# Elementwise work and the remainders of weights move from POOL to VectorE in a two-layer decoder trunk on one core

## Chip, cores and metric

One core of a Trainium2 chip runs the kernel alone. The metric is the device time of one launch in microseconds; what is shown is the median of the runs, and beside it one profiled execution with its own time.

## What is computed

One inference step of a trunk of two layers, for a prompt of 1024 tokens and a sample group of 8 x 4 tokens that share all weights. Layer 0 mixes by causal pooling and by sliding-window attention at three dilations, layer 1 by a chunked gMLP gate and a short convolution. Both then have a squared-ReLU MLP (1024 to 4096 to 1024) and a gated input embedding; norms are RMS norms in float32. Cut to what matters here:

```python
for i in range(DEPTH):                                    # DEPTH = 2
    h = rmsnorm(r, norm_mix[i])
    y = even_mixer(h, ...) if i % 2 == 0 else odd_mixer(h, ...)
    r = r + y
    h = rmsnorm(r, norm_ffn[i])
    r = r + square(relu(h @ ffn_w1[i])) @ ffn_w2[i]
    h = rmsnorm(r, norm_ple[i])
    r = r + sigmoid(h @ ple_w_gate[i]) * (p[i] @ ple_w_proj[i])
out = rmsnorm(r, norm_final)
# even_mixer: z = h @ w_in; q and k of each head get rope (x1*cos - x2*sin, x2*cos + x1*sin);
#   attention per dilation group, the three outputs combined by a softmax over their log-sums;
#   y = concat(pooled, attended) @ w_out
# odd_mixer: gelu gate, layer norm and 128-token spatial mix; g_out * conv3(g_in * xin); y = concat @ w_out
```

## The kernel before, in words

All 1056 tokens (1024 of the prompt, 32 of the sample) lie as columns, the features as eight tiles of 128 partitions. A float32 product is made of three passes of TensorE (PE): weights and activations are each split in a high part and a remainder, and the passes are high x high, high x remainder and remainder x high. For an activation the high part `sh` comes from ACT and the remainder `sl` from VectorE (DVE).

**The stream of weights.** `wseq` lists all weight tiles (128x1024) in the order of their use. `w_load` brings one to `wraw` (or to `wr`, where the MLP's weights are first combined for a Winograd-like scheme: L206 to L217 on DVE) by a DMA from SP's queue. `w_split(i)` lets ACT copy the tile rounded to `whi` (L153) and an elementwise engine make the remainder `wlo` = raw - high (L157), and then lets the next load start. `whi` and `wlo` have two buffers each. Before the change L157 stands on POOL (GpSimd) unless `eng` says DVE; in the MLP stages of layers 0 and 1 it stands on DVE two steps after the rounding. `w_ahead` splits the next weight while PE works on the present one, `w_next` takes it.

**Order.** Every engine runs its own instructions in the order in which the code issues them. A step of a product ends in `fill.step()`; `fill.after(n, f)` has `f` issued n steps later. That is how the other work is spread between the steps.

**Stages**, with their times in the profile: layer 0's mixer (0 to 770 us) with its tiles of q, k and v, the rope (`rope_tile`: cos on DVE at L490, sin by `pool_tt` at L284 on POOL, sum at L495 and remains for the sample at L497 and L499), and units of attention (`nmx`, L604, from the row maxima; ACT's exponential `p`, L607; PE's transposes `pt`, L626); the mixer's output product, which also leads into the MLP (770 to 866); the MLP of layer 0 (866 to 1454); its embedding and the input products of layer 1's mixer up to 1650; layer 1's mixer (1650 to 1900), which runs in the same code as an MLP does, in two products (`product1`, L1323, and `product2`, L1484); the lead and the MLP of layer 1 (to 2604); its embedding and the final norm.

In the lead of layer 0, `eo_part2(f)` runs eight times: nine matmuls, the sum `r` (DVE, L1120), the remainder `sl` of the tile before (DVE, L1142), then on ACT the rounding `sh` (L1137) and the square (L248), and the sum of squares `acc` (`prep_sq`: POOL for f = 1 to 6 at L284, DVE for f = 7 at L250). When `acc` is whole, PE sums it over partitions (L273).

In the final embedding `last_next` makes the same kind of sum (L1962), the projection's weight remainder `wpl` is DVE's (L1639), and `final_mul` multiplies by the norm's factor (L2009): of the first two thirds of the columns tiles 3 to 7 on POOL, of the last third tiles 5 to 7.

Of the kernel before, what the change touches and what calls it, by code (L numbers as in the profile page):

```python
# [11 lines left out]
F32 = mybir.dt.float32  # L12
# [45 lines left out]
def _build(nc, tc, A, top):  # L58
# [88 lines left out]
    def w_split(i, eng=None, later=False):  # L147
        if i >= len(wseq) or i in wsp:
            return
        w_raw(i)  # L150
        hi = wpool.tile([128, 1024], F32R, tag="whi", name=nm("whi"))
        raw, lo = wop[i]
        ACT.activation(hi, raw, AF.Copy)  # L153
        wsp[i] = (hi, lo)

        def rest():
            (eng or POOL).tensor_tensor(lo, raw, hi.bitcast(F32), op=ALU.subtract)  # L157
            if i not in wraw:
# [71 lines left out]
    def w_next():  # L230
        i = wptr[0]
        wptr[0] += 1
        w_split(i)
        return wsp[i]

    def w_ahead():
        w_split(wptr[0])
# [45 lines left out]
    def pool_tt(out, a, b, op):  # L283
        POOL.tensor_tensor(out, a, b, op=op)  # L284
# [84 lines left out]
    w_split(1, DVE)  # L369
# [8 lines left out]
    for f in (1, 2):  # L378
        pool_tt(xt[0], xt[0], xt[f], ALU.add)
# [65 lines left out]
    def norm0():  # L445
        tags = ("sA", "sB", "pt")
        norm_finish(lambda c: pa.tile([128, 512], F32, tag=tags[c], name=nm("nb")))
        DVE.tensor_tensor(cosr, cosr, rstd, op=ALU.mult)
        pool_tt(sinr, sinr, rstd, ALU.mult)

    def first_two():
# [4 lines left out]
        for t, k in [(t, k) for k in range(6) for t in range(2)] + [(0, 6), (0, 7), (1, 6), (1, 7)]:  # L456
# [7 lines left out]
            if (t, k) == (0, 7):  # L464
                w_split(2, DVE)
        return pss

    def rope_tile(hp, g, j, pss=None):
# [329 lines left out]
    def combine_items(hp):  # L798
# [274 lines left out]
    def gemm_phase(n, kslots, split, mid, evac, last=None, lead=None, chunks=None, skip=(), order=None,  # L1073
# [23 lines left out]
        w_split(wptr[0] + 1)  # L1097
        evac(1, p1)
        for f in range(2, n):
# [9 lines left out]
            if f not in skip:  # L1109
                w_split(wptr[0] + 1)  # L1110
# [60 lines left out]
    def pair(l, xslots, near, far, extra, gi, parts, more_slots, pieces, lead=None, order=None, spilled=False):  # L1171
# [53 lines left out]
        def sums_of(k):  # L1225
# [5 lines left out]
            def s0():  # L1231
                for f in (k, 4 + k):
                    ACT.activation(R[f], R[f], AF.Copy, scale=g[:, f:f + 1])
                POOL.tensor_tensor(raw7(k), c_, a_, op=ALU.subtract)
# [10 lines left out]
            def s3():  # L1245
                lows[5] = split_half(T5[k], a_, later=True)
                lows[3]()
                POOL.tensor_tensor(raw7(k), b_, a_, op=ALU.subtract)
# [61 lines left out]
        def product1(c, p):  # L1310
            w = w_next()
            first = PROD[p][0]
            for m in range(2):
# [12 lines left out]
                if m == 1:  # L1326
                    if (c, p) == (n1 - 1, 3):
                        second_open()
                    if l == "m":
                        w_split(wptr[0] + 1)  # L1330
# [33 lines left out]
        def after2(n, p, kt):  # L1364
# [5 lines left out]
            elif (p, kt) == (4, 1):  # L1370
                build(SD, H1, 1, range(P.early, 4))
                if n == 0:
                    minus(H0, 1, H1, 1, range(2), POOL)
# [4 lines left out]
            elif (p, kt) == (6, 0):  # L1378
                if n == 0:
                    minus(H0, 1, H1, 1, range(2, 4), POOL)  # L1380
# [92 lines left out]
        def product2(n, p, kt):  # L1473
# [3 lines left out]
            for i_m, m in enumerate(M_ORDER):  # L1477
# [10 lines left out]
                if l == "m":  # L1488
                    if m == 2 and not (last and p == 7 and kt == 1):
                        w_split(wptr[0] + 1)  # L1490
                elif i_m == 2 and not (last and p == 7 and kt == 1):
                    rest = w_split(wptr[0] + 1, DVE, True)
                    if rest:
                        fill.after(2, rest)
# [3 lines left out]
                if last and (p, kt, i_m) in pieces:  # L1498
                    ple_piece(*pieces[p, kt, i_m], POOL if l == "m" else DVE, xp, gi)
# [219 lines left out]
    def mix_parts(st):  # L1719
# [20 lines left out]
        def v_path(i, v, at):  # L1740
# [25 lines left out]
            def tr_s():  # L1766
                V.ps = mbank()
                PE.matmul(V.ps[:32, :128], v[:, NP:NT], C.cen, start=True, stop=True)
                POOL.tensor_tensor(C.wss[:, i, :], C.wss[:, i, :], C.smk, op=ALU.mult)
# [29 lines left out]
            def norm():  # L1799
                DVE.scalar_tensor_tensor(V.s, V.s, V.st[:32, 1, 8:9], V.g, op0=ALU.mult, op1=ALU.mult)  # L1800
                POOL.tensor_tensor(V.n, V.n, V.st[:, 1, 0:8].unsqueeze(2).to_broadcast([128, 8, 128]), op=ALU.mult)
# [4 lines left out]
            def offset():  # L1806
# [5 lines left out]
                POOL.tensor_tensor(V.s, V.s, V.o[:32, :], op=ALU.add)  # L1812
# [25 lines left out]
        def conv(i, hd, c, at, then):  # L1838
# [3 lines left out]
            def s0():  # L1842
                pool_tt(hd, hd, c, ALU.mult)
# [22 lines left out]
            def s4():  # L1866
                pool_tt(c, c, rstd, ALU.mult)
# [83 lines left out]
    def last_next(j):  # L1951
# [5 lines left out]
        else:  # L1957
# [4 lines left out]
            (DVE if f == 7 or (ch == ONE and f > 5) else POOL).tensor_tensor(acc[:, cs], acc[:, cs], sq[:, cs], op=ALU.add)  # L1962
        ACT.activation(r, r, AF.Copy, scale=gains[:, 6, f:f + 1])
        if j == 7:
# [4 lines left out]
            for i in range(8):  # L1969
                fill.after(39 + 1 * i, lambda i=i: final_mul(i, TWO, POOL if i in PO else DVE))  # L1970
# [49 lines left out]
    for i, f in enumerate((5, 0, 1, 6, 2, 3, 7, 4)):  # L2020
        if f >= 5:
            final_mul(f, ONE, POOL)
# [160 lines left out]
```

## Time and profile before

| | |
|---|---|
| median of the runs | 2777.39 us (2776.99 to 2777.65) |
| profiled execution, own time | 2770.68 us |
| its span in the profile | 2768.9 us |
| PE busy | 2650.0 us, 96% |
| DVE busy | 1780.0 us, 64%, 2542 instructions |
| ACT busy | 1118.0 us, 40% |
| POOL busy | 567.3 us, 20%, 270 instructions |

The profiled execution is 6.7 us shorter than the median; its trace is 1.8 us shorter than its own time. A line such as "650.00 1.96 DVE L495 ... [2.35 <-POOL tmp L284]" of the timeline says: start, duration, engine, line of the kernel, result and operands, and in brackets how long the engine had stood idle and what ended that. In the list of waits each line says which instructions of PE waited for which result, the total, how often, and the longest. PEclk is the granted clock of PE as a share of full speed.

### The profile page before, as it was taken

What the parts mean: (1) busy time and instruction counts of PE and PEld (TensorE: products, weight loads), DVE (VectorE), ACT (ScalarE), POOL (GpSimd) and SP (SyncE); (2) the same over time, 40 slices, a digit from 0 to 9 for tenths busy, and PEclk for the clock granted to TensorE, in tenths of its full rate; (3) what the DMA queues carried; (4) which work ended last, traced back from release to release, by engine and by line L of the source; (5) the groups of instructions that cost most, each with busy time, mean ns of one, the idle gap of its engine ahead of it and who ended that gap; (6) DMA issues with size and microseconds to landing.
All of it is one profiled execution on the core that took longest, in us unless ns stands there. A gap on an engine that the chain in (4) does not pass through costs nothing. (4 is left out here: it accounts for less than half of the span.)

```text
span 2768.9 us, 48732 instructions
## 1 busy us (share of the span) xinstructions
PE 2650.0 (96%) x20190; PEld 2563.8 (93%) x20190; DVE 1780.0 (64%) x2542; ACT 1118.0 (40%) x1901; POOL 567.3 (20%) x270
## 2 busy tenths in 40 slices
PE   8999999998989999999999999998999999999996
PEld 7898898987889999999999988988999999999996
DVE  7444435454377667777776465778866767777755
ACT  4333333334154333333354355224533343333543
POOL 3332233222251000000001334546400000000034
PEclk9999999999999999999999999999999999999998
DMA  5224334255644444744412222351254448443112
GB/s 172 75 87 130 105 107 147 84 155 157 193 170 166 138 147 154 278 168 156 148 56 79 77 87 89 88 172 47 85 179 157 149 174 293 135 139 132 55 63 103
DMA packets 159294, 366.52 MB, mean 132 GB/s; under 512 B 46528, under 2 KB 54752, under 8 KB 159072
## 3 DMA queue, kind: packets, MB, share of 16 engines
q1 hardware_dynamic: 158208, 362.59, 39.7%
q8 instruction: 159, 2.61, 0.4%
q10 hardware_dynamic: 864, 0.82, 0.1%
q14 instruction: 63, 0.52, 0.1%
HBM read 245.20 MB, written 105.15 MB: 127 GB/s over the span
## 5 line engine op out<-in xcount | busy, mean ns | idle before, releaser
L157 POOL TENSOR_TENSOR wlo<-wraw,whi 128x1024 fp32r<-128x1024 f32 x99 | 244.0, 2465 | 1875.3 <-ACT whi L153 1832.7
L1323 PE MATMUL PS<-sh,whi 128*128 128x264 f32 x2016 | 413.2, 286 | 17.3 <-DVE tmp L1305 4.8
L1323 PE MATMUL PS<-sh,wlo 128*128 128x264 f32 x2016 | 414.3, 287 | 5.9 <-POOL wlo L157 5.9
L1484 PE MATMUL PS<-sh,whi 128*128 128x264 f32 x2016 | 405.3, 283 | 14.2 <-DVE r L1497 12.8
L1323 PE MATMUL PS<-sl,whi 128*128 128x264 f32 x2016 | 413.9, 287 | 0.0
L1484 PE MATMUL PS<-sl,whi 128*128 128x264 f32 x2016 | 408.5, 284 | 1.2 <-DVE sl L1155 1.2
L1484 PE MATMUL PS<-sh,wlo 128*128 128x264 f32 x2016 | 409.4, 284 | 0.0
L1323 PEld LDWEIGHTS PS<-sh,whi 128*128 128x128 f32 x2016 | 318.1, 190 | 20.9 <-DVE tmp L1305 5.2
L1484 PEld LDWEIGHTS PS<-sh,whi 128*128 128x128 f32 x2016 | 313.8, 188 | 17.1 <-issue 11.0
L153 ACT ACTIVATE whi<-wraw 128x1024 fp32r<-128x1024 f32 x181 | 191.5, 1058 | 338.5 <-PE PS L1484 101.1
L1323 PEld LDWEIGHTS PS<-sh,wlo 128*128 128x128 f32 x2016 | 316.4, 191 | 6.9 <-POOL wlo L157 6.9
L153 ACT ACTIVATE whi<-wr 128x1024 fp32r<-128x1024 f32 x153 | 162.3, 1061 | 394.1 <-PE PS L1484 269.9
L1323 PEld LDWEIGHTS PS<-sl,whi 128*128 128x128 f32 x2016 | 315.0, 190 | 0.0
L421 PE MATMUL g<-sh,whi 128*128 128x352 f32 x888 | 310.2, 349 | 4.2 <-DVE vsn L532 3.0
L1484 PEld LDWEIGHTS PS<-sl,whi 128*128 128x128 f32 x2016 | 310.9, 188 | 1.8 <-DVE sl L1155 1.8
L1484 PEld LDWEIGHTS PS<-sh,wlo 128*128 128x128 f32 x2016 | 311.6, 189 | 0.0
L423 PE MATMUL g<-sh,wlo 128*128 128x352 f32 x888 | 287.5, 324 | 0.1
L422 PE MATMUL g<-sl,whi 128*128 128x352 f32 x888 | 287.0, 323 | 0.0
L157 DVE TENSOR_TENSOR wlo<-wr,whi 128x1024 fp32r<-128x1024 f32 x128 | 156.6, 1223 | 180.1 <-ACT whi L153 180.1
L421 PEld LDWEIGHTS g<-sh,whi 128*128 128x128 f32 x888 | 168.0, 189 | 25.8 <-issue 21.7
L1497 DVE TENSOR_TENSOR r<-r,PS 128x528 f32<-128x528 f32 x252 | 168.9, 698 | 21.1 <-PE PS L1484 21.1
L422 PEld LDWEIGHTS g<-sl,whi 128*128 128x128 f32 x888 | 168.9, 190 | 1.4
(341 smaller groups left out, 4593.3 us busy)
## 6 DMA issues: line engine op xcount, KB each, us to landing
hx<-hop SPq DMA_DIRECT2D x56, 528.0 KB, 4.7
tmp<-hop SPq DMA_DIRECT2D x56, 528.0 KB, 4.7
wr<-in_w SPq DMA_DIRECT2D x56, 512.0 KB, 3.7
hop<-tmp SPq DMA_DIRECT2D x96, 264.0 KB, 4.1
hop<-hx SPq DMA_DIRECT2D x96, 264.0 KB, 3.4
wr<-in_w1q SPq DMA_DIRECT2D x42, 512.0 KB, 4.0
wraw<-in_w_e SPq DMA_DIRECT2D x39, 512.0 KB, 3.4
rscr<-r SPq DMA_DIRECT2D x24, 528.0 KB, 3.2
```

The costliest lines, as they stand in the source:

```text
L153: ACT.activation(hi, raw, AF.Copy)
L157: (eng or POOL).tensor_tensor(lo, raw, hi.bitcast(F32), op=ALU.subtract)
L421: PE.matmul(ps[:, :CH], hi[:, ws], xh[:, cs], start=k == 0, stop=False)
L422: PE.matmul(ps[:, :CH], hi[:, ws], xl[:, cs], start=False, stop=False)
L423: PE.matmul(ps[:, :CH], lo[:, ws], xh[:, cs], start=False, stop=k == 7)
L1323: PE.matmul(ps[:, n, :], a[:, ws], b[:, n * HT // 2:(n + 1) * HT // 2], start=first and k == 0 and i == 0, stop=k == 3 and i == 2, skip_gr ...
L1484: PE.matmul(ps[:, q, :], a[:, ws], b[:, q * HT // 2:(q + 1) * HT // 2], start=first and kt == 0 and k == 0 and i == 0, stop=kt == 1 and k ...
L1497: DVE.tensor_tensor(r, r, ps, op=ALU.add)
```

## The change

Every elementwise instruction that `pool_tt` or POOL by name did in these stages is DVE's (`tt`), and so is every `wlo`. `w_split` gives its remainder back as a function; `w_soon(i, steps)` has it issued some steps after the rounding: four in layer 0's mixer, one in the leads, the output products and the embeddings, two in the two products of an MLP or of layer 1's mixer. `w_next` issues it if it is still due. In layer 1's mixer `product2` splits the next weight after the third block in its order (`i_m == 2`) as the other layers do. POOL keeps memsets and the small edges of the pooling (L916, L918): 34 of its 275 issued rows; DVE's grow from 2412 to 2654. PE's order is unchanged.

```diff
+    wrest = {}
+    def w_soon(i, steps=1):
+        rest = w_split(i, True)
+        if rest:
+            wrest[i] = rest
+            fill.after(steps, lambda: w_finish(i))
+    def w_finish(i):
+        if i in wrest:
+            wrest.pop(i)()
-    def w_split(i, eng=None, later=False):
+    def w_split(i, later=False):
...
         def rest():
-            (eng or POOL).tensor_tensor(lo, raw, hi.bitcast(F32), op=ALU.subtract)
+            DVE.tensor_tensor(lo, raw, hi.bitcast(F32), op=ALU.subtract)
...
         w_split(i)
+        w_finish(i)
         return wsp[i]
-    def w_ahead():
-        w_split(wptr[0])
+    def w_ahead(steps=1):
+        w_soon(wptr[0], steps)
...
             if f == 7 or eng is DVE:
                 DVE.tensor_tensor(acc, acc, sq, op=ALU.add)
             else:
-                pool_tt(acc, acc, sq, ALU.add)
+                tt(acc, acc, sq, ALU.add)
...
-    def pool_tt(out, a, b, op):
-        POOL.tensor_tensor(out, a, b, op=op)
+    def tt(out, a, b, op):
+        DVE.tensor_tensor(out, a, b, op=op)
...
             if c == 0 and k == 6:
-                w_ahead()
+                w_ahead(4)
...
             DVE.tensor_tensor(zs, zs, cosr, op=ALU.mult)
-            pool_tt(zw, zw, sinr, ALU.mult)
+            tt(zw, zw, sinr, ALU.mult)
...
                 if g == 1:
-                    pool_tt(ot, ot, st["cb"], ALU.mult)
+                    tt(ot, ot, st["cb"], ALU.mult)
...
-        w_split(wptr[0] + 1)
+        w_soon(wptr[0] + 1)
...
-                    if l == "m":
-                        w_split(wptr[0] + 1)
-                    else:
-                        rest = w_split(wptr[0] + 1, DVE, True)
-                        if rest:
-                            fill.after(2, rest)
+                    w_soon(wptr[0] + 1, 2)
...
-                    minus(H0, 1, H1, 1, range(2), POOL)
+                    minus(H0, 1, H1, 1, range(2))
...
-            (DVE if f == 7 or (ch == ONE and f > 5) else POOL).tensor_tensor(acc[:, cs], acc[:, cs], sq[:, cs], op=ALU.add)
+            DVE.tensor_tensor(acc[:, cs], acc[:, cs], sq[:, cs], op=ALU.add)
...
-                fill.after(39 + 1 * i, lambda i=i: final_mul(i, TWO, POOL if i in PO else DVE))
+                fill.after(39 + 1 * i, lambda i=i: final_mul(i, TWO, DVE))
...
         if f >= 5:
-            final_mul(f, ONE, POOL)
+            final_mul(f, ONE, DVE)
```

Left out of it: the same exchange at `sinr`, the squares of the input, L1234 and L1248 (`t7r`), L1769, L1801, L1812, the two products of the convolution's stages (L1843, L1867) and the sums of the embedding (L1607).

The order of DVE's instructions shows what comes behind what. In the changed kernel lines carry numbers some 14 higher in the middle of the file (L1120 is L1134 there, L1142 is L1156, L284 is L298, L1497 is L1501, L1155 is L1169, L1362 is L1371) and 4 higher near its end (L2009 is L2013).

DVE in the lead of layer 0, before, from the first sum on:

```order
L1120 TENSOR_TENSOR r_7356<-r_7356,PS 128x1056
L1120 TENSOR_TENSOR r_7357<-r_7357,PS 128x1056
L1142 SCALAR_TENSOR_TENSOR sl_83<-r_7356,gains,sh_82 128x1056
L1120 TENSOR_TENSOR r_7358<-r_7358,PS 128x1056
L1142 SCALAR_TENSOR_TENSOR sl_85<-r_7357,gains,sh_84 128x1056
L1120 TENSOR_TENSOR r_7359<-r_7359,PS 128x1056
L1142 SCALAR_TENSOR_TENSOR sl_87<-r_7358,gains,sh_86 128x1056
```

and now:

```order
L1134 TENSOR_TENSOR r_7356<-r_7356,PS 128x1056
L1134 TENSOR_TENSOR r_7357<-r_7357,PS 128x1056
L1156 SCALAR_TENSOR_TENSOR sl_83<-r_7356,gains,sh_82 128x1056
L298 TENSOR_TENSOR acc<-acc,tmp_7505 128x1056
L1134 TENSOR_TENSOR r_7358<-r_7358,PS 128x1056
L1156 SCALAR_TENSOR_TENSOR sl_85<-r_7357,gains,sh_84 128x1056
L298 TENSOR_TENSOR acc<-acc,tmp_7521 128x1056
L1134 TENSOR_TENSOR r_7359<-r_7359,PS 128x1056
L1156 SCALAR_TENSOR_TENSOR sl_87<-r_7358,gains,sh_86 128x1056
L298 TENSOR_TENSOR acc<-acc,tmp_7546 128x1056
```

Between the remainder of one tile and the sum of the next there is now the sum of squares, which before stood on POOL.

DVE in `product2` of layer 1's mixer, before:

```order
L1155 TENSOR_TENSOR sl_95<-hx_17056,sh_94 128x528
L1155 TENSOR_TENSOR sl_95<-hx_17089,sh_94 128x528
L1155 TENSOR_TENSOR sl_97<-tmp_17118,sh_96 128x528
L1155 TENSOR_TENSOR sl_97<-tmp_17149,sh_96 128x528
L1155 TENSOR_TENSOR sl_87<-hx_17480,sh_86 128x528
L1155 TENSOR_TENSOR sl_87<-hx_17513,sh_86 128x528
L1497 TENSOR_TENSOR r_17821<-r_17821,PS 128x528
```

and now:

```order
L1371 TENSOR_TENSOR hx_17480<-hx_17480,hx_17056 128x528
L1371 TENSOR_TENSOR hx_17511<-hx_17511,hx_17087 128x528
L1169 TENSOR_TENSOR sl_95<-hx_17056,sh_94 128x528
L1169 TENSOR_TENSOR sl_95<-hx_17087,sh_94 128x528
L1169 TENSOR_TENSOR sl_97<-tmp_17118,sh_96 128x528
L1169 TENSOR_TENSOR sl_97<-tmp_17147,sh_96 128x528
L170 TENSOR_TENSOR wlo_18096<-wraw_15733,whi_18097 128x1024
L1371 TENSOR_TENSOR tmp_17542<-tmp_17542,tmp_17118 128x528
L1371 TENSOR_TENSOR tmp_17571<-tmp_17571,tmp_17147 128x528
L1169 TENSOR_TENSOR sl_87<-hx_17480,sh_86 128x528
L1169 TENSOR_TENSOR sl_87<-hx_17511,sh_86 128x528
L1501 TENSOR_TENSOR r_17821<-r_17821,PS 128x528
```

One remainder of weights (L170) and four differences (`minus`, L1371, before L1362 on POOL) now stand in this piece of the line ahead of the sums `r`; another remainder stands a few rows ahead of the piece.

DVE in the last two jobs of the final embedding, before:

```order
L1962 TENSOR_TENSOR acc<-acc,tmp_26845 128x352
L2009 TENSOR_TENSOR r_22227<-r_22227,rs_25802 128x704
L1664 TENSOR_TENSOR tmp_26886<-PS,rstd 128x352
L1655 TENSOR_TENSOR tmp_26895<-PS,tmp_26886 128x352
L1656 TENSOR_TENSOR r_22232<-r_22232,tmp_26895 128x352
L1962 TENSOR_TENSOR acc<-acc,tmp_26898 128x352
```

and now:

```order
L1966 TENSOR_TENSOR acc<-acc,tmp_26845 128x352
L2013 TENSOR_TENSOR r_22227<-r_22227,rs_25802 128x704
L2013 TENSOR_TENSOR r_22228<-r_22228,rs_25802 128x704
L2013 TENSOR_TENSOR r_22229<-r_22229,rs_25802 128x704
L2013 TENSOR_TENSOR r_22230<-r_22230,rs_25802 128x704
L2013 TENSOR_TENSOR r_22231<-r_22231,rs_25802 128x704
L2013 TENSOR_TENSOR r_22232<-r_22232,rs_25802 128x704
L1668 TENSOR_TENSOR tmp_26886<-PS,rstd 128x352
L1659 TENSOR_TENSOR tmp_26895<-PS,tmp_26886 128x352
L1660 TENSOR_TENSOR r_22232<-r_22232,tmp_26895 128x352
L1966 TENSOR_TENSOR acc<-acc,tmp_26898 128x352
```

Five more of the final products of 704 columns stand between the last two jobs.

## Rows read from the trace of the kernel before

**Rows 1.** Head of the page: busy time, share and instructions of each engine.

```profile
PE 2650.0 (96%) x20190; PEld 2563.8 (93%) x20190; DVE 1780.0 (64%) x2542; ACT 1118.0 (40%) x1901; POOL 567.3 (20%) x270
```

**Rows 2.** Waits of PE over the whole span: total, times, longest.

```profile
PE PS L1484 <- DVE r L1497: 12.8, 7, 7.0
...
PE pt L626 <- ACT p L607: 7.7, 5, 3.3
...
PE pt L626 <- DVE pts L632: 5.1, 3, 3.7
PE PS L1323 <- POOL wlo L157: 5.9, 5, 1.7
...
PE PS L273 <- DVE acc L250: 4.5, 1, 4.5
...
PE g L1007 <- ACT sh L950: 3.8, 1, 3.8
...
PE g L756 <- DVE pts L747: 3.0, 1, 3.0
...
PE g L421 <- DVE vsn L532: 3.0, 1, 3.0
```

**Rows 3.** Groups by line, POOL and DVE: busy, mean ns of one, idle before.

```profile
L157 POOL TENSOR_TENSOR wlo<-wraw,whi 128x1024 fp32r<-128x1024 f32 x99 | 244.0, 2465 | 1875.3 <-ACT whi L153 1832.7 <-PE s L593 17.4 <-DVE rstd L281 8.4
...
L157 DVE TENSOR_TENSOR wlo<-wraw,whi 128x1024 fp32r<-128x1024 f32 x82 | 100.3, 1224 | 34.6 <-ACT whi L153 32.5
...
L279 DVE TENSOR_TENSOR acc<-tmp 128x1056 f32<-128x1056 f32 x6 | 7.6, 1259 | 24.1 <-ACT tmp L277 24.1
```

**Rows 4.** Timeline of POOL and DVE in layer 0's mixer, at 250 and 650 us.

```profile
249.84 2.34 POOL L157 TENSOR_TENSOR wlo<-wraw,whi 128x1024 fp32r<-128x1024 f32 x1 [4.79 <-ACT whi L153]
...
250.25 1.95 DVE L604 TENSOR_SCALAR nmx<-mlt 128x2 f32<-128x2 f32 x1
...
252.91 0.17 DVE L604 TENSOR_SCALAR nmx<-mlt 128x2 f32<-128x2 f32 x1
...
646.39 1.26 DVE L490 TENSOR_TENSOR tmp<-tmp,cosr 128x1056 f32<-128x1056 f32 x1 [0.41 <-DMA tmp<-tmp]
650.00 1.96 DVE L495 TENSOR_TENSOR k<-tmp,tmp 128x1024 f32<-128x1024 f32 x1 [2.35 <-POOL tmp L284]
651.81 2.29 DVE L499 TENSOR_TENSOR ksn<-tmp,tmp 128x32 f32<-128x32 f32 x1
```

**Rows 5.** Timeline of POOL, DVE and ACT in the lead of layer 0.

```profile
779.96 6.49 POOL L284 TENSOR_TENSOR acc<-acc,tmp 128x1056 f32<-128x1056 f32 x2 [4.57 <-ACT tmp L248]
...
790.93 1.24 DVE L1120 TENSOR_TENSOR r<-r,PS 128x1056 f32<-128x1056 f32 x1
...
792.21 1.18 ACT L1137 ACTIVATE sh<-r,gains 128x1056 fp32r<-128x1056 f32 x1 [1.30 <-DVE r L1120]
793.29 1.07 ACT L248 ACTIVATE tmp<-r 128x1056 f32<-128x1056 f32 x1
...
800.23 3.38 DVE L250 TENSOR_TENSOR acc<-acc,tmp 128x1056 f32<-128x1056 f32 x1 [2.34 <-POOL acc L284]
```

**Rows 6.** Timeline of DVE in product2 of layer 1's mixer.

```profile
1856.56 1.33 DVE L1155 TENSOR_TENSOR sl<-acc,sh 128x528 fp32r<-128x528 f32 x2
...
1868.54 4.24 DVE L1155 TENSOR_TENSOR sl<-tmp,sh 128x528 fp32r<-128x528 f32 x2
...
1880.72 3.46 DVE L1155 TENSOR_TENSOR sl<-hx,sh 128x528 fp32r<-128x528 f32 x2
```

**Rows 7.** Timeline of DVE at the end of the final embedding and behind it.

```profile
2737.38 1.97 DVE L1639 TENSOR_TENSOR wpl<-wpr,wph 128x256 fp32r<-128x256 f32 x1 [1.52 <-ACT wph L1638]
...
2741.30 3.74 DVE L2009 TENSOR_TENSOR r<-r,rs 128x704 f32<-128x704 f32 x2
...
2754.43 0.53 DVE L1656 TENSOR_TENSOR r<-r,tmp 128x352 f32<-128x352 f32 x1
```

**Rows 8.** Window behind a gap of PE: length, PE busy, granted clock, DMA share, GB/s.

```profile
253.20:256.60 3.40, 3.35 (x14) 0.51 0.66 227
```

More of the change, by code (lines that the diff above doesn't have):

```diff
@@ L368, in _build @@
     split_w0(slice(wcut, 1024))
-    w_split(1, DVE)
+    w_split(1)
     for f in range(1, 8):
@@ L378, in _build @@
     for f in (1, 2):
-        pool_tt(xt[0], xt[0], xt[f], ALU.add)
+        tt(xt[0], xt[0], xt[f], ALU.add)
     for f in (4, 5, 6, 7):
@@ L448, in norm0 @@
         DVE.tensor_tensor(cosr, cosr, rstd, op=ALU.mult)
-        pool_tt(sinr, sinr, rstd, ALU.mult)
+        tt(sinr, sinr, rstd, ALU.mult)
     def first_two():
@@ L464, in first_two @@
             if (t, k) == (0, 7):
-                w_split(2, DVE)
+                w_split(2)
         return pss
@@ L1109, in gemm_phase @@
             if f not in skip:
-                w_split(wptr[0] + 1)
+                w_soon(wptr[0] + 1)
             evac(f, ps)
@@ L1233, in s0 @@
                     ACT.activation(R[f], R[f], AF.Copy, scale=g[:, f:f + 1])
-                POOL.tensor_tensor(raw7(k), c_, a_, op=ALU.subtract)
+                DVE.tensor_tensor(raw7(k), c_, a_, op=ALU.subtract)
             def s1():
@@ L1247, in s3 @@
                 lows[3]()
-                POOL.tensor_tensor(raw7(k), b_, a_, op=ALU.subtract)
+                DVE.tensor_tensor(raw7(k), b_, a_, op=ALU.subtract)
             return s0, s1, s2, s3, lambda: lows[5]()
@@ L1328, in product1 @@
                         second_open()
-                    if l == "m":
-                        w_split(wptr[0] + 1)
-                    else:
-                        rest = w_split(wptr[0] + 1, DVE, True)
-                        if rest:
-                            fill.after(2, rest)
+                    w_soon(wptr[0] + 1, 2)
                 evac1(c, p, m, ps)
@@ L1379, in after2 @@
                 if n == 0:
-                    minus(H0, 1, H1, 1, range(2, 4), POOL)
+                    minus(H0, 1, H1, 1, range(2, 4))
                     build(SA, H0, 0, range(P.early))
@@ L1487, in product2 @@
                     fill.step()
[L1488 to L1494, printed above, removed]
+                if i_m == 2 and not (last and p == 7 and kt == 1):
+                    w_soon(wptr[0] + 1, 2)
                 if kt == 1:
@@ L1498, in product2 @@
                 if last and (p, kt, i_m) in pieces:
-                    ple_piece(*pieces[p, kt, i_m], POOL if l == "m" else DVE, xp, gi)
+                    ple_piece(*pieces[p, kt, i_m], DVE, xp, gi)
             if l == "m":
@@ L1768, in tr_s @@
                 PE.matmul(V.ps[:32, :128], v[:, NP:NT], C.cen, start=True, stop=True)
-                POOL.tensor_tensor(C.wss[:, i, :], C.wss[:, i, :], C.smk, op=ALU.mult)
+                DVE.tensor_tensor(C.wss[:, i, :], C.wss[:, i, :], C.smk, op=ALU.mult)
             def square_s():
@@ L1800, in norm @@
                 DVE.scalar_tensor_tensor(V.s, V.s, V.st[:32, 1, 8:9], V.g, op0=ALU.mult, op1=ALU.mult)
-                POOL.tensor_tensor(V.n, V.n, V.st[:, 1, 0:8].unsqueeze(2).to_broadcast([128, 8, 128]), op=ALU.mult)
+                DVE.tensor_tensor(V.n, V.n, V.st[:, 1, 0:8].unsqueeze(2).to_broadcast([128, 8, 128]), op=ALU.mult)
             def mask():
@@ L1811, in offset @@
                 DVE.tensor_tensor(C.off, V.b, ps[:, :128], op=ALU.add)
-                POOL.tensor_tensor(V.s, V.s, V.o[:32, :], op=ALU.add)
+                DVE.tensor_tensor(V.s, V.s, V.o[:32, :], op=ALU.add)
                 SP.dma_start(out=A["cv"][:, 128 * i:128 * i + 128], in_=V.s)
@@ L1842, in s0 @@
             def s0():
-                pool_tt(hd, hd, c, ALU.mult)
+                tt(hd, hd, c, ALU.mult)
                 E.x = C.op.tile([128, 8, 6], F32, tag="cext", name=nm("cext"))
@@ L1866, in s4 @@
             def s4():
-                pool_tt(c, c, rstd, ALU.mult)
+                tt(c, c, rstd, ALU.mult)
                 then()
```

## The prediction

> **What bounds the kernel now.** I begin with the head of the page: PE is busy for 2650.0 us of 2768.9, so 118.9 us are all that its gaps hold, and a change that leaves PE's work alone can only win from these gaps and from the clock behind them [rows 1]. DVE has 64%, so there is room for more on the whole; what counts is where it stands in line. Next come the waits of PE, to see which gaps end with an engine that the change touches [rows 2]: the sums r of the second product, 12.8 us; the exponentials p, 7.7; wlo from POOL, 5.9; the copies pts (L632), 5.1; acc in the lead, 4.5; sh of L950, 3.8; pts (L747) and vsn, 3.0 each. Together that is 45.8 us.
>
> The timelines tell why DVE and ACT are late there. At 250 us POOL makes a wlo from 249.84 on; DVE's tiny nmx, 0.17 us when alone, starts at 250.25 and ends with POOL's instruction, 1.95 us later, and ACT's p waits for it. At 650 us k waits 2.35 us for POOL's sine product, and then k and a piece of 128x32 take 1.96 and 2.29 us with the next wlo beside them [rows 4]. In layer 1's mixer pairs of sl take 4.24 to 3.46 us, where a pair alone takes 1.33 [rows 6]. A DVE instruction with its operands in SBUF thus stands still while a POOL instruction runs; one that reads PSUM does not, as r with 1.24 us beside POOL's squares [rows 5].
>
> The third thing to see is the clock: behind such a gap PE's granted clock is 0.5, its lower level of 1.2 GHz, for 3.4 us, as from 253.2 to 256.6 [rows 8]. 3.4 us of work at half speed cost 1.7.
>
> **The change part by part.** It removes 241 instructions from POOL, most of its 567.3 us. A wlo costs 2465 ns there and 1224 on DVE; a tile of 128x1056 costs 1259 on DVE [rows 3]. The 124 wlo give 152 us to DVE, some 47 tiles of 128x1056 another 59, the smaller ones about 50: DVE gets 261 us, and gets back what it stood still behind POOL. PE and ACT lose and gain nothing themselves; SP's loads of weights move past one or two others, and those loads are issued a tile or more ahead of use, so I cost this at nothing; without that cover ACT's rounding would wait for its load and PE for that, and no wait of PE in its list ends with a load.
>
> Layer 0's mixer, to 770 us:
> - Three gaps before p, 7.7 us with two more: nmx no longer stands behind a wlo, 1.78 us at 250, somewhat less at the other two. I take 4.6; at least 0, at most 7.7.
> - 650 us: cosine and sine products follow each other on DVE from 646.39 on: 1.26 + 1.26 + 1.22 for k (a tile of 1024 columns) + 0.17 for a piece as small as nmx end at 650.3, where that piece ends at 654.1 now [rows 3, 4]. The gap behind it is 3.7 long [rows 2]: -3.7; bounds 0 and -3.7.
> - sh of L950 waits for ACT, which was held up by an nmx under a wlo as above: -1.7 of 3.8. pts of L747 waits behind a product on ot of POOL and one of DVE that stands behind a wlo: -3.0 of 3.0. vsn: the first rope loses its standstill but DVE gets two sine products, one on the tables and a wlo (5.0 us): -2 of 3.0.
> - The clock: four stretches at half speed come behind these gaps (at 65.5, 253.2, 676.5 and 751.6 us; the third has twice the length), 1.7 us each or more; half of that goes: -4 (0 to -8).
> - New waits in line: a wlo whose whi is late holds up all of DVE behind it. The 82 wlo that DVE makes now waited 32.5 us for ACT, 0.40 each [rows 3]; 124 more make 49 us of idle DVE. The steps between rounding and remainder (four here) are there to cover this, and where they don't, PE must first run out of work. I let one eighth reach PE, 6 us, 3 of it here. Bounds: 0, and all 49.
> Sum here -16.
>
> The lead of layer 0. Now POOL's squares run beside r and sl; the first starts at 779.96, and the last sum, on DVE, ends at 800.23 + 3.38 = 803.6, for which PE waits 4.5 us [rows 2, 5]. After the change acc(f) stands in line ahead of r(f+1), and waits for the square of f, which ACT starts only behind r and sh of f: 1.24 + 1.18 + 1.07 + 1.26 less some 0.1 of overlap, 4.65 us per tile. From 779.96 six tiles and one acc end at 809.1: **+5.5**, less 0.5 for a shorter wlo behind it: +5. If ACT were ahead, DVE alone would need 3 x 1.25 = 3.75 per tile, ending at 803.7: 0. With the clock at half speed for longer it may be +9.
>
> product2 of layer 1's mixer. Four pairs of sl take some 15.4 us for 5.3: 10 us come back. In their line now stand two wlo and four differences, 2 x 1.22 + 2 x 1.33 = 5.1 [rows 3, 6]. The gap of 7.0 us before the sums r [rows 2] gets shorter by 5 (0 to 7). Here a page says something else: the Trainium skill, "GPSIMD Engine Reference", section 3.1, has an elementwise instruction with two inputs 1.96 times as long on GpSimd as on VectorE. By that ratio alone the two wlo at 2465 ns become 2.5 us on DVE and nothing comes back: the gap would grow by them, and by the differences too. The sum goes by the rows, in which DVE has been paying for POOL's time already.
>
> Elsewhere: the other six waits for r, 5.8 us, -3 (0 to -5.8). Gaps that end with POOL's wlo, 5.9 us, five times: a wlo is 1.24 us shorter but stands in DVE's line, -3.5 (0 to -5.9). The clock behind the gaps of layer 1's mixer, at 1840.4 and, of twice the length, 1881.4 us: -2.5. Waits in line: +3.
>
> The final embedding and the end. wpl, 128x256, takes 1.97 us behind a wlo [rows 7] and by its columns (1024 take 1224 ns) some 0.4 alone: 1.5 come back per job of one third of the columns. DVE gets that job's acc and wlo, 1.8 us, of which half fits in its waits for ACT (1.52 before this wpl): 0.6 shorter, four jobs, -2.4. Products with the norm's factor: two take 3.74 us beside POOL's; alone I put one at 0.89, two thirds of 1259 ns and its start [rows 3], and six of the eight now stand in one row ahead of the last job, 5.3 us; from 2741.3 to the last acc I get 14.0 us in place of 15.0, -1. Behind the last sum three products on 128x352 at 0.53 [rows 7] join DVE's five, which ran beside POOL's: +1.4. Sum -2 (-5 to +3).
>
> **Sum:** -16 + 5 - 5 - 3 - 3.5 - 2.5 + 3 - 2 = -24. The MLP stages have no POOL instruction and stay. The profiled execution took 2770.68 us (span 2768.9), so it becomes 2746.7; the median stands 6.7 higher, and I forecast **2753 us**.
>
> **The rivals.**
> - *PE takes the next wait instead.* A gap that ends later with the next late thing gives back half. PE's 96% speak for it, and that many gaps have ACT behind DVE. By the Trainium skill, "Perfetto Trace Analysis", section Identifying the Most-Contended Engine, one works first on the engine with the highest occupancy; that is PE, and the change adds to another one. Worked from rows: gains of 16 us (half of 32), the lead's +5 and the waits' +3: -8, 2769 us; -3 to -13 with the waits' size. What speaks against it: the gaps of rows 2 end with just those instructions that stand behind POOL.
> - *More comes back.* All waits of rows 2 but acc go, 41 us, the clock keeps its level behind them (-10), less the lead's 5: -45, 2732 us. It needs the in-line waits to cost nothing.
> - *Slower.* One mechanism: the line of DVE. A wlo whose whi is not ready stops r, sl and nmx behind it, and PE waits for them. Without waits in line the sum is -30. With all 49 us reaching PE it is +19, 2796 us; it decides from 30/124 = 0.24 us per wlo on. For it: in the same way 32.5 us were lost on DVE before. Against it: there they cost PE nothing that its list of waits shows, and the steps let the rounding finish.
> - That the change doesn't do what it says is ruled out by the order: POOL keeps 34 rows, and DVE has 242 more.
>
> **How the numbers follow.** The measurement can tell 0.2%, 5.6 us, from no change. Forecast 0.60 (2743 to 2763 by the bounds of its larger terms), the first rival 0.19, more 0.14, slower 0.07. Faster by over 0.2%: 0.60 + 0.14 + 0.12 of the first rival = 0.86; within 0.2%: its other 0.07; slower: 0.07. The range reaches from 2733, which leaves out the lower half of "more", to 2770, which leaves out "slower" and the weak end of the first rival: together some 0.2.
>
> **What would show it.** Right: POOL under 10 us; nmx and ksn near 0.17 us everywhere; the gaps at 252.9, 654.5, 751.4 and 1885 gone, with fewer stretches at half clock; in the lead a pace of 4.65 us per tile and a longer wait of PE for acc; DVE at about 1860 us busy. Wrong: PE's waits for r or nmx as long as before, now behind a wlo that waits for ACT; or a lead at 3.8 us per tile; or waits for wlo that add up to over 10 us.

## The result, and the profile after

| | before | changed |
|---|---|---|
| median of the runs with the first result | 2777.19 us (2776.31 to 2777.65) | 2740.41 us (2734.84 to 2743.53) |
| ratio to before, 95% interval | | 0.9866 [0.9849, 0.9883] |
| profiled execution, span / own time | 2768.9 / 2770.68 us | 2738.1 / 2739.92 us |

The kernel got faster, 37 us by these medians, 31 by the two traces; 24 were forecast, and the time lies in the range. Both kernels were run again later, and before with the other experiments too: its medians then were 2773.0 to 2775.4, and the change gave 2744.70, 0.9896 [0.9881, 0.9911]. The gain is thus some 28 to 37 us; single times of either kernel spread by 5 to 17 us.

The head of the page of the changed kernel, which answers to [rows 1]:

```profile
PE 2642.0 (96%) x20190; PEld 2559.8 (93%) x20190; DVE 1834.7 (67%) x2783; ACT 1118.9 (41%) x1901; POOL 15.0 (1%) x29
```

POOL lost 552 us, and DVE, which took over all that work, gained only 55. I had put the work at 261 us of DVE; in the changed trace the durations of the 241 moved instructions add up to 261 us as well. The durations of all of DVE's instructions grew by 74 us, so those that DVE had before got 187 us shorter: that much of what DVE was busy with before was standing still. The instructions that read PSUM did not change: the 252 sums r of the second products (128x528) took 698 ns before and 697 now. PE idled for 118.9 us before and for 96.1 now (span less busy), and its busy time, with the same matmuls, fell by 8.0 us: the stretches at half clock add up to 77 us before and 57 now.

The list of PE's waits, against [rows 2] (line numbers are some 14 higher):

```profile
PE PS L1493 <- DVE r L1501: 7.6, 9, 1.7
PE PS L1987 <- DVE acc L1966: 7.4, 1, 7.4
PE PS L317 <- DVE r L1134: 7.3, 4, 2.9
PE PS L317 <- DVE wlo L170: 7.0, 5, 2.1
PE g L437 <- DVE wlo L170: 6.3, 1, 6.3
...
PE PS L287 <- DVE tmp L288: 2.6, 1, 2.6
PE g L1021 <- ACT sh L964: 2.2, 1, 2.2
PE pt L640 <- ACT p L621: 2.2, 2, 1.5
...
PE pt L640 <- DVE pts L646: 1.2, 2, 0.7
...
PE PS L287 <- DVE acc L264: 1.0, 1, 1.0
```

Gone or smaller are the gaps behind r of the second product (12.8 to 7.6, the one of 7.0 with them), p (7.7 to 2.2), pts (5.1 to 1.2; the 3.0 of L747 and the 3.0 of vsn are not in the list any more) and sh (3.8 to 2.2). The wait for acc in the lead fell from 4.5 to 1.0. New are 7.3 us behind r in the lead and 13.3 behind remainders that DVE makes; the 5.9 us behind POOL's remainders are gone.

PE issues the same 20190 matmuls in the same order in all kernels here, so the start of the same matmul can be set against the trace of before. The stretches in which the difference moves are the places where time goes. In us, for the matmul that starts at the given time in the first trace of before:

| at | before, 2nd trace | change | change, 2nd | only remainders | only the others | old split | mended |
|---|---|---|---|---|---|---|---|
| 50 | -0.5 | +7.5 | +8.6 | +9.8 | +0.5 | +7.2 | -0.7 |
| 100 | -0.7 | -0.2 | +1.2 | +2.6 | -1.7 | -0.8 | -6.9 |
| 751 | +4.3 | -16.3 | -14.1 | -6.0 | -6.1 | -14.1 | -20.3 |
| 775 | +5.5 | -17.6 | -12.8 | -7.5 | -6.1 | -14.0 | -21.0 |
| 825 | +5.1 | -10.7 | -6.3 | -6.7 | +1.7 | -6.0 | -21.6 |
| 870 | +5.3 | -14.7 | -10.4 | -6.8 | -3.5 | -10.1 | -25.5 |
| 1650 | +5.0 | -13.7 | -10.9 | -1.8 | -6.9 | -8.6 | -27.3 |
| 1850 | +4.4 | -21.1 | -18.7 | -4.5 | -10.6 | -17.7 | -34.4 |
| 1900 | +5.5 | -29.3 | -26.9 | -13.4 | -12.2 | -20.0 | -42.6 |
| 2025 | +3.8 | -31.0 | -28.4 | -10.2 | -12.0 | -21.9 | -42.2 |
| 2600 | +3.9 | -31.0 | -28.4 | -10.2 | -11.9 | -20.5 | -40.8 |
| 2756 | +5.5 | -30.6 | -28.0 | -11.2 | -12.8 | -18.6 | -46.9 |

Two traces of one kernel differ by up to 5 us, in steps of about 1.5: one more or one fewer stretch of PE at its lower clock behind a gap. A place counts where several traces agree. The columns on the right are experiments told below; each has one trace, and three of these are of executions longer than their kernel's median: 2759.45 us for "only remainders" (2754.35), 2751.91 for "old split" (2749.92) and 2723.45 for "mended" (2719.41).

### The profile page after: what moved, and what is told of

Same layout as the page of the kernel before. It is cut to its first block, busy times and chain, and to the rows that moved or that the text cites. A ratio compares the mean times of both kernels' runs of the same rounds, so it can differ in the third digit from the quotient of the medians.

```text
span 2738.1 us, 48467 instructions
## 1 busy us (share of the span) xinstructions
PE 2642.0 (96%) x20190; PEld 2559.8 (93%) x20190; DVE 1834.7 (67%) x2783; ACT 1118.9 (41%) x1901; POOL 15.0 (1%) x29
## 4 chain that ended last, share of the span: by engine, by line
PE 47%; DVE 6%; ACT 3%; issue 1%; DMA 1%; SPq 0%; DVEq 0%; ACTq 0%
PE PS L1493 24%; PE PS L1337 14%; PE PS L317 8%; DVE sl L1169 1%; DVE wlo L170 1%; DVE r L1501 1%; DMA r<-rscr 0%; ACT whi L166 0%; ACT sh L1166 0%; ACT sh L271 0%; PE PS L287 0%; DMA wr<-in_w_m 0%; ACT PS L1767 0%; DMA wr<-in_w1q_m 0%; DVE r L2013 0%
## 5 line engine op out<-in xcount | busy, mean ns | idle before, releaser
L170 DVE TENSOR_TENSOR wlo<-wr,whi 128x1024 fp32r<-128x1024 f32 x153 | 187.0, 1222 | 194.5 <-ACT whi L166 194.5
L170 DVE TENSOR_TENSOR wlo<-wraw,whi 128x1024 fp32r<-128x1024 f32 x181 | 221.0, 1221 | 46.6 <-ACT whi L166 43.8
L435 PEld LDWEIGHTS g<-sh,whi 128*128 128x128 f32 x888 | 167.8, 189 | 21.1 <-issue 18.5
L1501 DVE TENSOR_TENSOR r<-r,PS 128x528 f32<-128x528 f32 x252 | 168.8, 697 | 15.1 <-PE PS L1493 15.1
L317 PE MATMUL PS<-sh,whi 128*128 128x352 f32 x696 | 163.3, 331 | 12.6 <-DVE r L1134 7.3
```

Of the source, the lines that this page charges most:

```text
L170: DVE.tensor_tensor(lo, raw, hi.bitcast(F32), op=ALU.subtract)
L317: PE.matmul(ps[:, :CH] if one else ps[:, c, :CH], a[:, ws], b[:, c * CH:(c + 1) * CH], start=start and i == 0, stop=stop and i == 2)
L1501: DVE.tensor_tensor(r, r, ps, op=ALU.add)
```

## The experiments

**The two kernels once more.** Nothing is edited in either.

> The changed kernel once more, for the spread of its times and a second trace. Theory (VectorE's waits behind POOL are refunded): about 2740 us, and the same place-by-place differences to the kernel before as in the first trace: some -16 us up to 751 us, +3 across the lead of layer 0, -16 in layer 1's mixer. Rival (the gain is chance of one execution): places differ by more than 3 us between the two traces.

> The kernel before once more, for a second trace. Its first profiled execution was 6.7 us shorter than the median of its runs. Theory: the profiled execution of this kernel was one with other clock levels behind gaps, and another trace shows a time nearer 2777 with the difference in stretches at half clock. Rival: profiling itself shortens this kernel by 6.7 us, and the second trace reads 2769 again.

The change gave 2744.70 us (2742.5 to 2747.45). Its two traces agree by place within 1.5 us but for steps of the clock before 100, at 250 and at 775 us (the largest 2.6). Before gave 2775.79 us (2769.64 to 2786.6) and a span of 2774.3, so profiling doesn't shorten it by 6.7 us; the first trace was a short one of a wide spread. Its second trace has 24 us at half clock before 770 us, the first 17.

**Which half of the move counts.** In the first kernel `tt` and all other places but L157's are POOL's again; in the second they are DVE's and the kernel is otherwise the one before.

```diff
 only remainders, from the change:
-        DVE.tensor_tensor(out, a, b, op=op)
+        POOL.tensor_tensor(out, a, b, op=op)
 only the others, from the kernel before:
-        POOL.tensor_tensor(out, a, b, op=op)
+        DVE.tensor_tensor(out, a, b, op=op)
...
```

> Only the remainders of weights are VectorE's (with the new steps); all other elementwise work is back on POOL. Theory (waits behind POOL): the gaps behind nmx and in product2 come mostly from POOL's remainders, so most of the gain stays, 2755 us (2748 to 2762), and the lead keeps its old pace of 3.4 us per tile; sl pairs in product2 of layer 1's mixer still stand behind the two pairs of differences on POOL. Rival A (a remainder is simply ready sooner): only the waits of PE that ended with POOL's remainder go, 6.6 us, about 2771. Rival B (the earlier split in product2 and the steps make the gain): all of it stays, about 2740.

> Only the other elementwise work is VectorE's; the remainders of weights are POOL's at the old places. Theory: VectorE still stands behind 124 remainders, and POOL's remainders behind VectorE; about 2768 us (2760 to 2774), nmx still up to 1.9 us, the lead at 4.65 us per tile. Rival A: the same or slower than before, 2777 to 2785, since VectorE only gets more work. Rival B: 2777.

2754.35 us, 0.9934 [0.9919, 0.9949], and 2760.63 us, 0.9954 [0.9937, 0.9970]. The remainders alone give 19 us and the rest 12, together 31 where the change gave 28 beside them: the theory's size fits the first; the second gained 12 us where 9 were expected and lies at the near end of its range. Rival A falls with both: the first gained 19 us where it had 6.6, and the second only gave DVE more work and got faster. Rival B falls with both too, as neither gains all or nothing; but the first kernel keeps the earlier split, so a part of its 19 us is the split's (8.9 of them lie from 1850 to 1900 in the table, see below). Of the pairs of sl in the first kernel's `product2` one still stood beside POOL's differences (1.65 and 1.83 us); the others took 0.70 us each. The table shows two prices apart. The loss of 8 us before 50 comes with the remainders, the loss from 775 to 825 with the others, where the sums of squares are: +7.7 there, +0.8 in the first kernel.

**POOL back, as an extra.** The changed kernel with an idle POOL made to work again. First POOL makes each moved remainder before DVE makes it again; then it writes as long, without reading more than 8 columns.

```diff
         ACT.activation(hi, raw, AF.Copy)
 reads:
+            POOL.tensor_tensor(lo, raw, hi.bitcast(F32), op=ALU.subtract)
 writes:
+            POOL.tensor_copy(lo[:, :8], hi[:, :8].bitcast(F32))
+            for _ in range(20):
+                POOL.memset(scr, 0.0)
+            POOL.tensor_copy(lo[:, :8], hi[:, :8].bitcast(F32))
```

> The changed kernel, but POOL also makes every moved remainder into the same tile first, and VectorE makes it again over it: POOL reads and runs some 2.4 us per weight as before, VectorE has its full new work, and a remainder is ready later by POOL's time. Theory (a POOL instruction that reads SBUF makes VectorE's instructions on SBUF stand still): nmx up to 1.9 us and the sl pairs up to 4 us again, 2775 to 2795 us. Rival (only the price of work matters, POOL beside costs nothing but the later remainder): nmx 0.17, 2745 to 2755.

> The changed kernel, but per moved remainder POOL first copies 8 columns of the rounded weight into the remainder's tile, sets a 128x16 scratch tile 20 times to zero (some 2.2 us that only write) and copies the 8 columns again; then VectorE makes the whole remainder over them. The remainder is ready as late as in the run where POOL reads. Theory (it is POOL's reading that stops VectorE): nmx stays at 0.17 us, 2743 to 2756. Rival (any POOL instruction stops VectorE): as the run where POOL reads, 2770 or more.

2844.67 us, 1.0245 [1.0223, 1.0268], and 2834.65 us, 1.0209 [1.0189, 1.0228]. Both times were missed, the first by 50 us and the second by 80. As time tests they fail, for a reason worth having: DVE's own remainder now waits for POOL's, and all of DVE's line behind it. DVE's list of waits in the run that writes:

```profile
DVE wlo L176 <- ACT whi L167: 218.8, 132, 3.6
DVE wlo L176 <- POOL wlo L173: 166.3, 67, 5.7
```

With 166 us of a stopped line the kernel is 90 us slower (2834.65 against 2744.70). That is the mechanism of my slower rival, at about half a us per us in this one run. The durations do answer the question. nmx of 96 pieces had 236 ns on the mean where POOL reads, 171 where it writes in short pieces; the projection's remainders, with POOL reading and with POOL writing:

```profile
L1645 DVE TENSOR_TENSOR wpl<-wpr,wph 128x256 fp32r<-128x256 f32 x22 | 21.9, 1004 | 20.5 <-ACT wph L1644 20.5
```

```profile
L1649 DVE TENSOR_TENSOR wpl<-wpr,wph 128x256 fp32r<-128x256 f32 x22 | 9.2, 424 | 20.5 <-ACT wph L1648 20.5
```

**The same without the stopped line.** POOL's extra work now comes behind DVE's remainder, into the raw tile, which nobody reads again.

```diff
             DVE.tensor_tensor(lo, raw, hi.bitcast(F32), op=ALU.subtract)
+            if i in wraw and 2 < i < len(wseq) - 8:
 reads:
+                POOL.tensor_tensor(raw, raw, hi.bitcast(F32), op=ALU.subtract)
 writes:
+                POOL.memset(raw, 0.0)
+                POOL.memset(raw, 0.0)
+                POOL.memset(raw[:, :512], 0.0)
```

> The changed kernel, and behind each remainder whose raw weight came by its own load (98 weights; not those from the MLP's combinations) POOL once more subtracts the rounded weight from the raw one, into the raw tile, which nobody reads again; only the load that reuses that tile waits for it. VectorE's order and work are those of the change. Theory (VectorE's instructions on SBUF stand still while POOL reads SBUF): the gaps behind nmx and the rope come back in part, nmx up to 2 us, 2752 to 2768 us. Rival (POOL beside VectorE costs nothing, the gain comes from cheaper and earlier instructions): as the change, 2738 to 2746.

> The same place and about the same length on POOL, but POOL only writes: it sets the raw tile to zero twice and half of it a third time. Theory: no standstill, nmx at 0.17 us, 2738 to 2750 (a few us for the later loads). Rival (any POOL instruction stops VectorE): as the run in which POOL reads.

2788.17 us, 1.0052 [1.0038, 1.0066], and 2756.91 us, 0.9937 [0.9923, 0.9950]; it applied to 72 weights, not 98. Both are slower than expected (at most 2768 and 2750). The next load into the raw tile now waits for POOL on SP's queue. The row of SP's waits in the second trace of the change, and in the second run:

```profile
SPq L129 <- DVE wlo L170: 456.2, 57, 50.0
```

```profile
SPq L129 <- POOL wraw L174: 595.8, 59, 56.8
```

DVE's wait for a transfer (cr) in the second run, which is 6.4 and 3.2 us in the second trace of the change:

```profile
DVE cw L853 <- DMA cr<-mscr: 14.3, 4, 5.1
...
DVE cw L855 <- DMA cr<-mscr: 4.8, 8, 1.7
```

That the late loads hold up cr is read from these rows and not tested by a run of its own. This part is about the same in both (613.0 us of SP's waits where POOL reads, 20.9 us of waits for cr). The difference between them, 31.3 us for 72 weights, is reading (2.9 us each, with POOL's own waits) against writing (2.4 us in three). The heads of their pages, reading and then writing; the change's second trace has DVE at 1835.2:

```profile
PE 2662.1 (96%) x20190; PEld 2573.9 (92%) x20190; DVE 1900.3 (68%) x2783; ACT 1118.4 (40%) x1901; POOL 225.1 (8%) x101
```

```profile
PE 2649.0 (96%) x20190; PEld 2565.2 (93%) x20190; DVE 1836.6 (67%) x2783; ACT 1119.0 (41%) x1901; POOL 190.7 (7%) x245
```

DVE runs the same 2783 instructions in both and is busy 64 us longer where POOL reads. The groups of DVE's small instructions show what stood still. In the changed kernel, with POOL reading, with POOL writing:

```profile
L618 DVE TENSOR_SCALAR nmx<-mlt 128x2 f32<-128x2 f32 x96 | 16.2, 169 | 3.3
...
L513 DVE TENSOR_TENSOR ksn<-tmp,tmp 128x32 f32<-128x32 f32 x11 | 2.1, 188 | 0.0
```

```profile
L620 DVE TENSOR_SCALAR nmx<-mlt 128x2 f32<-128x2 f32 x96 | 30.4, 317 | 3.3
...
L515 DVE TENSOR_TENSOR ksn<-tmp,tmp 128x32 f32<-128x32 f32 x11 | 23.8, 2160 | 0.0
```

```profile
L622 DVE TENSOR_SCALAR nmx<-mlt 128x2 f32<-128x2 f32 x96 | 24.1, 251 | 3.6
...
L517 DVE TENSOR_TENSOR ksn<-tmp,tmp 128x32 f32<-128x32 f32 x11 | 2.1, 193 | 0.0
```

ksn, a sum of two tiles, takes 188 ns alone, 2160 on the mean with POOL reading and 193 with POOL writing; in both runs ten of the eleven lie beside a POOL instruction. Where POOL reads, it stands still. For nmx the theory's 0.17 us failed: POOL's writing alone held it up too, to 251 ns on the mean, less than reading did.

**The earlier split in layer 1's mixer.**

```diff
-                if i_m == 2 and not (last and p == 7 and kt == 1):
+                if (m if l == "m" else i_m) == 2 and not (last and p == 7 and kt == 1):
```

> The changed kernel with layer 1's mixer splitting the next weight behind block number 2 (the fourth in its order), as before the change, in place of the third. Theory: the gain there comes from POOL's absence, within 3 us of the change, 2737 to 2746. Rival (the earlier split makes the gain in product2): the 12 us of product2 are lost again, 2750 or more.

2749.92 us, 0.9908 [0.9894, 0.9921]. That is 5 us behind the change at its second running, 9.5 behind the first, and just outside the expected range: the theory alone is not enough. By place, 6.8 us of it lie between 1850 and 1925 in the trace of before, where PE waits for remainders, which it doesn't there in the change. PE's waits in the stretch of product2, with the old split and in the change's second trace:

```profile
PE PS L1493 <- DVE wlo L170: 7.0, 3, 3.7
PE PS L1493 <- DVE r L1501: 0.6, 1, 0.6
```

```profile
PE PS L1493 <- DVE r L1501: 3.5, 3, 1.8
```

A remainder that stands in DVE's line has to be issued earlier than one on an idle POOL. The rival is real in a part: of the 8 us that the change gains from 1850 to 1900 the old split keeps 2.3, and of the 16 us from 1650 to 1900 it keeps 11.4.

**Mending places.** Three runs edit the change further: one step in place of four in layer 0's mixer; the lead's sum of squares one tile later; and both kinds of edit together with two more.

```diff
 mixer, one step:
-                w_ahead(4)
+                w_ahead(1)
 lead, one tile later:
             prep_lo(f - 1)
+            lead_acc(f - 1)
...
 all four (mixer only for the first weights):
+                w_ahead(1 if wptr[0] <= 4 else 4)
         w_ahead()
+        w_finish(wptr[0])
         evac(0, p0)
...
     fill.flush()
+    two_out(4)
+    two_out(5)
     rows_a(ONE)
     diag_mul(0)
+    two_out(6)
+    two_out(7)
```

`lead_acc(f)` adds the square of tile f, which ACT has made in `prep_hi`; `two_out(i)` is the last product of tile i on two thirds of the columns and its transfer out; tiles 0 to 2 stay where they were, tile 3 is issued behind the last r.

> The changed kernel with one step in place of four between rounding and remainder in layer 0's mixer. Theory (at 47.6 us PE waits 6.3 us for a remainder that stands in VectorE's line behind the norm and the first products of the rope, though its rounding is long done): the remainder stands ahead of the norm, the wait is gone and the first 100 us are 3 to 6 us shorter; elsewhere in the mixer a remainder may now stop nmx while it waits for ACT, +0 to +3. About 2739 us against 2743 of the change. Rival (four steps are needed, VectorE stands behind ACT's rounding): the mixer gets slower by 3 us or more.

> The changed kernel with the sum of squares of a tile one tile later in VectorE's line in the lead of layer 0 (r of f+1, sl of f, then acc of f). Theory (acc waits for ACT's square and holds up r): the pace falls from 4.64 us per tile to 3.8 or PE's own 3.4, and the lead gets 5 to 6 us shorter, about 2738. Rival (VectorE's busy time is the limit, or PE gets its work later for another reason): less than 2 us.

> The changed kernel with four places mended: the first remainders of layer 0's mixer one step behind the rounding (others four), the lead's sum of squares one tile later, the remainder ahead of the first evacuation of each product with a norm issued at once, and five of the eight last products on two thirds of the columns moved behind the last job's r, acc or norm. Theory (each of the four waits is VectorE's order): -5, -5.5, -3 and -4 against the change by the places in the trace, 2722 to 2730. Rival (the next wait takes each place): less than half, 2733 or more.

One step: 2738.30 us, 0.9863 [0.9843, 0.9883]. At 50 us it is 8.3 us ahead of the change's first trace, at 100 it keeps 4.3 of them; but gaps before p and pts are there again (1.7 at 70 us, 1.8 at 230, 1.6 at 557), and at 751 nothing is left of the gain (-15.8 against -16.3 and -14.1). So one step is better for the first weights and four for the others; the rival is right in a part, and the median's 2 to 6 us lie within the spread of the change.

Lead: 2737.96 us, 0.9859 [0.9837, 0.9882]. From 751 to 803 us the lead is 6.4 us shorter than in the change's first trace and 8.8 than in its second, more than expected. The timeline of DVE in the change, and then in this run:

```profile
776.34 1.26 DVE L298 TENSOR_TENSOR acc<-acc,tmp 128x1056 f32<-128x1056 f32 x1 [0.99 <-ACT tmp L262]
777.51 1.25 DVE L1134 TENSOR_TENSOR r<-r,PS 128x1056 f32<-128x1056 f32 x1
778.68 1.31 DVE L1156 SCALAR_TENSOR_TENSOR sl<-r,gains,sh 128x1056 fp32r<-128x1056 f32 x1
780.98 1.26 DVE L298 TENSOR_TENSOR acc<-acc,tmp 128x1056 f32<-128x1056 f32 x1 [0.99 <-ACT tmp L262]
```

```profile
773.64 1.25 DVE L1167 TENSOR_TENSOR acc<-acc,tmp 128x1056 f32<-128x1056 f32 x1
774.81 1.25 DVE L1134 TENSOR_TENSOR r<-r,PS 128x1056 f32<-128x1056 f32 x1
775.97 1.31 DVE L1171 SCALAR_TENSOR_TENSOR sl<-r,gains,sh 128x1056 fp32r<-128x1056 f32 x1
777.20 1.25 DVE L1167 TENSOR_TENSOR acc<-acc,tmp 128x1056 f32<-128x1056 f32 x1
```

780.98 less 776.34 is the pace of 4.64 us per tile, with DVE idle for 0.99 while ACT makes the square; now it is 777.20 less 773.64, 3.56, and DVE doesn't wait.

All four: **2719.41 us**, 0.9802 [0.9789, 0.9815], better than both kernels and than the expected 2722 to 2730: 54 us ahead of before, 21 to 25 ahead of the change. By place against the change's second trace: -8.1 up to 100 us, -7.8 in the lead, -2.1, -2.0 and -2.4 in three products with a norm (the second gives 2.7 back right behind), -4.0 in the last jobs; about what each was expected to give, and the rival falls. Its list of PE's waits no longer has DVE's wlo near its head, and acc at the end is at 3.4 in place of 7.4:

```profile
PE PS L1509 <- DVE r L1517: 7.6, 9, 1.7
PE g L476 <- ACT sh L271: 6.0, 3, 4.6
...
PE PS L2005 <- DVE acc L1984: 3.4, 1, 3.4
```

## Why the prediction was right, point by point

- **What bounded the kernel.** Right. PE has 96% before and after; 23 of the 31 us between the traces came out of gaps that ended with DVE, with ACT behind DVE's standstill or with POOL's remainders, and 8 out of the clock behind them. POOL's reading is shown to be the cause for sums of two tiles (the last pair of runs with POOL's extra work); for nmx its writing has a part. The Trainium skill, "GPSIMD Engine Reference", section 3.1, has a two-input elementwise instruction 1.96 times as long on GpSimd as on VectorE, and wlo agrees (2465 and 1224 ns). By that ratio alone an estimate is that POOL's 552 us make DVE some 280 us busier. DVE is 55 us busier; the measurement decides for the rows.
- **Layer 0's mixer: -16.** -16.3 and -14.1. The total was right and its parts were not all: nmx, the rope at 650, sh and pts moved as put ([rows 4] had nmx at 1.95; it is 169 ns on the mean and at most 172 now; of the gap at 252.9, which was to go, 1.5 and 1.9 of 3.3 us are left, while those at 654.5 and 751.4 went from 3.7 to 0.5 and from 3.0 to nothing), but a wait of 6.3 us at 47.6 us was new:

```profile
53.95 0.66 PE L437 MATMUL g<-sh,wlo 128*128 128x352 f32 x1 [6.32 <-DVE wlo L170]
```

  I had named the wait in line, but sized it at 3 us spread over the mixer. It stood in one place, in DVE's line behind the norm and the first products of the rope, though its rounding was done; it was given back by 100 us, as the first rope ended 4.3 us earlier (vsn starts at 59.46 in place of 63.73) and the gap of 1.4 before p at 77 was gone. That the total of -16 was met is thus in part luck: this one wait was twice the 3 us put for the whole mixer, and the first rope gave back more than the 2 us put.
- **The lead: +5.** The mechanism and the pace were right: 4.64 us per tile against 4.65, and acc ended 791.5 less 758.2 = 33.3 us behind the start of r(1), where 809.1 less 775.8 = 33.3 was put. By the matmuls the stretch from 775 to 803 lost 5.5 and 5.2 us. Two things were not as put. PE's wait for acc did not get longer: it fell from 4.5 to 1.0 and 0.4 us, because PE had already lost the time at r (7.3 us) and came to acc late. And some 4 us came back between 825 and 870, where in the kernel before PE waited 1.7 us for POOL's wlo and 1.1 for whi, for which the sum had 0.5. From 751 to 870 the lead cost 1.6 and 3.7 us. Longer half clock, for which +9 was held possible, is not what the traces show: from 751 to 870 there are 13.6 us of it before, 6.8 and 13.6 in the change.
- **product2 of layer 1's mixer: -5**, and with the waits for r, the clock and the wlo there some -10. The pairs of sl take 1.32 us each now, as put, and the sums r follow at once:

```profile
1854.25 1.32 DVE L1169 TENSOR_TENSOR sl<-hx,sh 128x528 fp32r<-128x528 f32 x2
1855.49 1.93 DVE L1501 TENSOR_TENSOR r<-r,PS 128x528 f32<-128x528 f32 x3
```

  The gap of 7.0 us before these sums is 1.7 now, so the -5 was met, but not for the reason of the sum alone. From 1650 to 1900 the traces have -15.7 and -16.0. Here a term failed: the earlier split had no price in my sum at all, though the diff shows it. With the old split the stretch gains 11.4, near the -10 put, and in product2 the gap behind r goes to nothing while the remainders come 7.0 us too late for PE: there the refund alone moves PE to its next wait. That the -5 came out is in this part luck.
- **Waits in line elsewhere, +3.** They are +2.0 behind 1475, +1.4 behind 1600 and +4.0 (in the second trace +2.4) behind 2625 us of before, in all three places a remainder behind DVE's evacuation, most of the 7.0 us in the list of PE's waits; more than I put. With the 6.3 in layer 0's mixer the waits for wlo add up to 13.3 us: this is over the 10 that I had named as a sign of being wrong, and the time came out well all the same, since more came back elsewhere. The size of a wait was put too high and its weight too low: DVE's waits for ACT ahead of wlo grew from 212.6 to 238.3 us, 0.21 for each of the 124 where the sum had 0.40. The 0.40 was also read too narrowly: the row in [rows 3] is that of the raw tiles, and 128 more remainders, from `wr`, were DVE's already and waited 180.1 us.
- **The end, -2.** -3.2 from 2733 us on; acc's wait fell only from 8.9 to 7.4, as the six products in a row stand ahead of it. The page's own time fell to 2739.92, 6.8 below my 2746.7: that is the mixer of layer 1, some 6, and the lead, which cost less than put. The median fell by another 6, since the profile of before was at the short end of its runs; the offset of 6.7 that I added did not belong to the changed kernel, whose profile is at its median.
- **Rivals.** "PE takes the next wait" is not what happened on the whole: the gaps closed. In product2 it is what happens with the old split. "More comes back" was nearer for layer 1's mixer. The slower rival's mechanism exists (the first pair of POOL's extra work, and the wait at 47.6), but 0.21 us of waiting for each of the 124 remainders stays just below the 0.24 from which it would decide.
- **The other signs.** POOL has 15.0 us where under 10 was named, DVE 1835 where some 1860 was; ksn takes at most 197 ns.

## What to carry to other kernels

An engine's work can stop its neighbour, as POOL's did VectorE's here, so look at the durations of the neighbour's smallest instructions beside it: a 0.17 us instruction that takes 2 shows what the other engine takes away, and what moving its work refunds to it (187 us here, of which 28 to 37 came out of the kernel's time). After such a move order is the price: a result that came from an idle engine whenever it was ready now has a place in a line, and must be issued ahead of what it would otherwise wait behind, and behind nothing that waits itself. Follow each gap to its matmul; four edits of a few lines, each found so, gave another 21 to 25 us here.

## What was not expected of the hardware

A POOL instruction that only writes let sums of two tiles run (ksn 193 ns) but not nmx, a TENSOR_SCALAR: up to 937 ns beside memsets of 954 ns, 251 on the mean, where 20 short ones of 111 ns left it at 171. The Trainium skill, "SBUF — State Buffer", section Who interferes with whom, says this: a VectorE instruction with two inputs in SBUF contends with GpSimd's reads and not with its writes, and tensor_scalar can take the pair of ports that VectorE shares with GpSimd; the durations here agree. The standstill goes both ways: of the 72 reading instructions that POOL was given behind DVE's remainders, 26 took 2.67 us or more (up to 7.76), and at the start of each of these DVE was busy with an instruction on two SBUF tiles; the other 46 took at most 2.41, and at the start of none of them was DVE so. And where a load waited for POOL, unrelated transfers on SP's queue came later: DVE's waits for cr were 19.1 us against 9.6.
